# Other accumulator banks, another pool order, another tail, and another DMA queue in a hybrid encoder trunk

## The chip, the cores and the metric

The kernel runs on one core of one Trainium2 chip. The metric is the device time of one execution in microseconds. The time before is the median of three runs, 2415.16 us (2414.27 to 2418.61). TensorE does the matrix products, VectorE (DVE) and ScalarE (ACT) the elementwise work, GpSimd (POOL) small copies and stores, SyncE (SP) only requests transfers. A transfer is requested on the queue of one of SP, ACT or POOL and stands in that queue's order.

## The reference, cut to what matters

The input is 1024 frames of 1024 channels in float32, and there are two layers.

- Layer 0: RMSNorm, one input projection `w_in` (26 column tiles of 128), an RWKV-7 time-mixing group (8 heads of 64, a recurrence over time) beside a chunked band attention (8 heads of 64, softmax with a relative bias), both concatenated and mapped by `w_out`, residual; then RMSNorm, `square(relu(h @ up)) @ down` with 4096 hidden channels, residual.
- Layer 1: RMSNorm, pointwise product with GLU, causal depthwise convolution of 31 taps, LayerNorm, swish, pointwise product, residual; then the same MLP with other weights.
- A final RMSNorm: each frame is divided by the root mean square of its 1024 channels, times a gain per channel.

## The kernel before, in words

The sequence is cut into two halves of 512 frames, `h` = 0 and 1. Activations are kept transposed (128 channels by 512 frames, eight tiles `x` per half). Every float32 operand of a dense product is split into a rounded high part and the remainder (`wh`, `wl` of a weight; `xh`, `xl` of an activation), and each 128x128x512 step is three matmuls: high by high, low by high, high by low.

A dense weight goes through `weight_raw` (L247): a tile `wr` of 256 KB (four 128-row blocks of 128 columns, that is 512 B runs in memory; for the value projection 128 rows of 512 columns) with 4 buffers, requested on SP's queue. `weight_part` (L254) then makes `wh` on ACT (L258) and `wl` on DVE (L259), from a pool with 4 buffers each in the first part of the kernel (`wp1`) and 8 each in the later part (`wp2`). Such a half weight feeds 12 matmuls. `gemm` (L268) runs output tiles through the banks tagged `d`; L144 is the one line that issues every dense matmul.

The value projection is at the end of `w_in_gemm` (L397): its four output tiles of 128 frames each are held in four PSUM banks at once while `k` runs over eight weight tiles (L422 on). The banks' tags are in `SPARE`: d, d, a, a. The eight banks of the first part are d (2), w (2), v (1), c (1) and a (2). Tag `a` belongs to the attention, `c` holds the state of the RWKV recurrence for the whole of `rwkv(h)`, and `v` is used in passing by its second stage.

Order of the work: `w_in_gemm(0)`; then the mixed stage, in which `rwkv(0)` and `attention(0)` are laid between the dense steps of `w_in_gemm(1)`, and `rwkv(1)` and `attention(1)` between those of `mixer_out(0)` and `ffn(0)` of layer 0; then the wide part, whose products take two output tiles at a time (`wide[0]`) on five `d` banks: layer 0 for half 1, the convolution module and the MLP of layer 1 for both halves. The mixers hand their data on through DRAM: `pd`, `ph`, `pl`, `vd` from the projection, `yd` with their outputs, stored on POOL's queue and read on SP's. The small scratch transfers of the recurrence (`msc`, `nb`, `xsc`, `xdt`) and the attention's loads (`kk`, `qq`, `ql`, `vt`, `bias`) are on SP's queue too, between the weights.

The instruction order of each engine and queue is fixed when the program is built: a list scheduler takes instructions by priority ("support" first, then "mixer", "attn", "dense") against estimated costs. What runs later than it estimated is waited for in that order. Dense matmuls come in runs (L149 on, `run_of`), of 6 in the projections.

SBUF pools are stacked. A pool opened later at the same address waits, tile by tile (`reuse_waits="tile"`), for those that used it. The wide part opens `wp2` first, so its 32 KB per partition lie where `lop` and `wp1` and the first of `mp` (the MLP's intermediate tiles `mh`, `ml`) lay.

The tail is class `Out` (L1043). For each finished output tile `m`, `add` scales by the final gain (L1053), transposes back through bank `o` (L1059) and copies into row tiles `u` (L1065, L1067). The squares are summed on the way (`Stat.add`, L214: square on ACT, sum on DVE). In the last half the last tile comes in two column halves, and after each `write` (L1074) sums over channels by matmul (L1079), takes root (L1082) and reciprocal (L1083), scales the row tiles alternately on DVE (L1091) and ACT (L1089), and sends them out on SP's queue (L1092).

Of the kernel before, what the change touches and what calls it, by code (L numbers as in the profile page):

```python
# [64 lines left out]
def encoder_trunk(ctx: ExitStack, tc: tile.TileContext, x, vecs, consts, ext, w2a2, g2, w_in, w_out,  # L65
                  up0, dn0, pw1, pw2, up1, dn1, out):
    nc = tc.nc
# [8 lines left out]
    dram = ctx.enter_context(tc.tile_pool(name="dram", bufs=1, space=bass.MemoryType.DRAM))  # L76
    ps = {}
    wide = [False]
    wb = [None]
    extra = [None]  # L80
    deferred = []

    def psum(tag):
        return ps[tag].tile([P, T], F32, tag=tag, name=tag)
# [89 lines left out]
    def boost():  # L174
        return At("support")
# [4 lines left out]
    def tmp(tag="t1"):  # L180
        return dpool.tile([P, T], F32, tag=tag, name=tag)
# [65 lines left out]

    def weight_raw(src, n, queue=None):
        raw = wpool.tile([P, KH, P], F32, tag="wr", name="wr", bufs=4)
        (queue or nc.sync.dma_start)(raw[:].rearrange("p a b -> p (a b)").rearrange("p (k n) -> p k n", n=n),  # L250
                                     src.rearrange("(k p) n -> p k n", p=P))
        return raw

# [146 lines left out]
    def w_in_gemm(h, rhs, st, first=()):  # L400
        def evac(m, q, cols):
            rstd = st.rstd()
            s = tmp("t1")
            if Q0 <= m < K0:
                nc.vector.scalar_tensor_tensor(out=s[:], in0=q[:], scalar=0.125, in1=rstd[:],
                                               op0=ALU.mult, op1=ALU.mult)
            else:
                nc.vector.tensor_tensor(out=s[:], in0=q[:], in1=rstd[:], op=ALU.mult)  # L408
            ts = slice(h * T, (h + 1) * T)
            if Q0 <= m < V0:  # L410
                hi = tmp("t2")
                nc.scalar.copy(hi[:].bitcast(F32R), s[:])
                nc.vector.tensor_tensor(out=s[:].bitcast(F32R), in0=s[:], in1=hi[:], op=ALU.subtract)
                nc.gpsimd.dma_start(ph[m][:, ts], hi[:])
                stored[h, m] = nc.gpsimd.dma_start(pl[m][:, ts], s[:])
            else:
                stored[h, m] = nc.gpsimd.dma_start(pd[m][:, ts], s[:])

        run_of(RUN[0])
        gemm(w_in, 0, IN_ORDER, rhs, evac, st, first, mark=h)  # L420
        run_of(RUN[2])
        qs = [psum(tag) for tag in SPARE]  # L422
        for k in range(KT):
            with boost():
                hi, lo = (a[:].rearrange("p a b -> p (a b)")
                          for a in weight_part(w_in[k * P : (k + 1) * P, V0 * P : V0 * P + RW], RW))
            xh, xl = rhs[k]
            for t, q in enumerate(qs):
                ts = slice(t * P, (t + 1) * P)
                dense(q[:], xh[:, ts], hi, start=(k == 0), stop=False)  # L430
                dense(q[:], xl[:, ts], hi, start=False, stop=False)
                dense(q[:], xh[:, ts], lo, start=False, stop=(k == KT - 1))
        with boost():
            for t, q in enumerate(qs):
                s = tmp("t1")
                nc.scalar.activation(s[:], q[:], AF.Copy, scale=st.part[1][:, t : t + 1])
                nc.gpsimd.dma_start(vd[h * T + t * P : h * T + (t + 1) * P, :], s[:])
# [481 lines left out]

        gemm(w, row0, range(KT), rhs, evac, taper=taper, after=after, halves=halves)  # L920

    def norm_collect(xs, gname):
        st = Stat()
        rhs = [None] * KT

        def last(m, cols):
            if gname is not None:
                rhs[m] = split(xs[m][:], m, v(gname, m))
            st.add(xs[m][:], cols)

        return st, rhs, last

# [9 lines left out]
        return nrhs, st  # L942

    def ffn(xs, rhs, rst, up, dn, mp, nxt, out_to=None, late=None):
        st, nrhs, last = norm_collect(xs, nxt)
        if out_to is not None:
            out_to.st = st
        groups = DFF // D
        mids = [[None] * KT for _ in range(groups)]
        ahead = 2 if wide[0] else 0  # L950

        def evac(m, q, cols):
            rstd = rst.rstd()
            t = tmp("t1")
            nc.vector.scalar_tensor_tensor(out=t[:], in0=q[:], scalar=0.0, in1=rstd[:], op0=ALU.max, op1=ALU.mult)  # L955
            sq = tmp("t2")
            nc.scalar.activation(sq[:], t[:], AF.Square)  # L957
            hi = mp.tile([P, T], F32R, tag="mh", name="mh")
            nc.scalar.activation(hi[:], t[:], AF.Square)  # L959
            lo = mp.tile([P, T], F32R, tag="ml", name="ml")  # L960
            nc.vector.tensor_tensor(out=lo[:], in0=sq[:], in1=hi[:].bitcast(F32), op=ALU.subtract)  # L961
            mids[m // KT][m % KT] = (hi, lo)

        done = 0
        for grp in range(groups):
            end = grp == groups - 1
            if late is not None and end:
                with At("mixer"):
                    late()
# [75 lines left out]
    class Out:  # L1045
# [5 lines left out]
        def add(self, m, cols):  # L1051
            n = tmp("t1")
            nc.scalar.activation(n[:, cols], self.xs[m][:, cols], AF.Copy, scale=v("gf", m))  # L1053
            q = psum("o")
            c2, j = divmod(m, 4)
            ts = range(cols.start // P, cols.stop // P)
            for t in ts:
                with At("dense"):
                    nc.tensor.transpose(q[:, t * P : (t + 1) * P], n[:, t * P : (t + 1) * P], ident)  # L1059
            for t in ts:  # L1060
                if self.o[4 * c2 + t] is None:
                    self.o[4 * c2 + t] = self.op.tile([P, T + TAPS - 1], F32, tag="u", name="u", bufs=8)
                dst, src = self.o[4 * c2 + t][:, j * P : (j + 1) * P], q[:, t * P : (t + 1) * P]
                if t % 2:
                    nc.vector.tensor_copy(dst, src)  # L1065
                else:
                    nc.scalar.copy(dst, src)  # L1067
            if self.final and m == KT - 1:
                self.write(ts)

        def finish(self):
            with boost():
                self.write(range(4))

        def write(self, ts):
            q = psum("o")
            for t in ts:
                with At("dense"):
                    nc.tensor.matmul(q[:, t : t + 1], self.st.acc[:, t * P : (t + 1) * P], ones[:, 0:1], start=True, stop=True)  # L1079
            w = slice(ts[0], ts[-1] + 1)  # L1080
            r = self.r
            nc.scalar.activation(r[:, w], q[:, w], AF.Sqrt, bias=kc[:, 0:1], scale=1.0 / D)  # L1082
            nc.vector.reciprocal(out=r[:, w], in_=r[:, w])  # L1083
            for c2 in range(2):
                for t in ts:
                    rows = slice(self.h * T + t * P, self.h * T + (t + 1) * P)
                    o = self.o[4 * c2 + t][:, 0:T]
                    if t % 2:
                        nc.scalar.activation(o, o, AF.Copy, scale=r[:, t : t + 1])  # L1089
                    else:  # L1090
                        nc.vector.tensor_scalar(o, o, r[:, t : t + 1], None, op0=ALU.mult)  # L1091
                    nc.sync.dma_start(out[rows, c2 * T : (c2 + 1) * T], o)  # L1092


    with banks(d=2, w=2, v=1, c=1, a=2), tc.tile_pool(name="lop", bufs=1) as lop, tc.tile_pool(name="wp1", bufs=4) as wb[0]:
# [43 lines left out]

        with ExitStack() as es:  # L1140
            rp, ap, lp = (es.enter_context(tc.tile_pool(name=n, bufs=1, reuse_waits="tile")) for n in ("rp", "ap", "lp"))
            with At("mixer"):
                rwkv(0, rp, 3)
            with At("attn"):
                attention(0, ap)
            w_in_gemm(1, reload_x(1, lp), sb)
# [11 lines left out]

    wide[0] = True
    run_of(1)  # L1160
    with banks(d=5, w=1, o=2), tc.tile_pool(name="wp2", bufs=8, reuse_waits="tile") as wb[0], tc.tile_pool(name="mp2", bufs=10, reuse_waits="tile") as mp, tc.tile_pool(name="sx", bufs=4, reuse_waits="tile") as extra[0], tc.tile_pool(name="up", bufs=1, reuse_waits="tile") as up:
        dwt = up.tile([P, KT * TAPS], F32, tag="dwt", name="dwt")
        nc.scalar.dma_start(dwt[:], vecs[:, VOFF["dw"] : NVEC])
        halo = up.tile([P, KT, TAPS - 1], F32, tag="halo", name="halo")
# [92 lines left out]
```

## Time and profile before

| | us |
|---|---|
| median of three runs | 2415.16 |
| the profiled execution, its own time | 2409.59 |
| its span, first to last instruction | 2407.5 |
| TensorE busy | 2374.8 |
| VectorE busy | 1706.2 |
| ScalarE busy | 1198.9 |
| GpSimd busy | 117.1 |

The mean granted clock of TensorE is 0.998 of full speed. The profile is of one execution; the row views below are all taken from it. A busy TensorE still may run at half clock or with gaps that pipelining hides, so stretches are best compared by how many dense matmuls they hold.

### The profile page before, as it was taken

The page shows a single profiled execution, that of the slowest core. Times are in us where ns is not written, and L with a number is a line of the kernel's source. Part 1 is how long each engine was busy: PE and PEld are TensorE (multiplying, and loading weights), DVE is VectorE, ACT ScalarE, POOL GpSimd, SP SyncE. Part 2 cuts the span into 40 slices and gives each one's busy share as a digit, 9 for nine tenths or more (in the row PEclk, how much of TensorE's full clock was granted, in tenths as well). Part 3 has the DMA queues.
Part 4 walks back from the last instruction along what each step waited for, and adds up shares of the span by engine and source line. Part 5 has one row for each costly group of instructions (what it writes and reads, how often), then busy time and mean ns, then how long its engine had stood idle before and what let it go on. Part 6 is the DMA issues. An engine that isn't in the chain of part 4 may idle for free.

```text
span 2407.5 us, 37122 instructions
## 1 busy us (share of the span) xinstructions
PE 2374.8 (99%) x12804; PEld 1956.4 (81%) x12804; DVE 1706.2 (71%) x3575; ACT 1198.9 (50%) x2323; POOL 117.1 (5%) x243
## 2 busy tenths in 40 slices
PE   9999999899999999999999999999999999999998
PEld 7777777788888888888888888888888888888887
DVE  6787776587777764579999746799997465434434
ACT  6567666677676753434433335334333365423324
POOL 1120111100000000011000000000000000000000
PEclk9999999999999999999999999999999999999999
DMA  8574445633343323453333334433333334333332
GB/s 260 163 217 139 120 121 171 188 102 115 93 120 110 90 74 90 145 166 92 101 97 97 97 97 135 123 94 97 96 98 99 95 112 140 97 97 97 97 98 67
DMA packets 476042, 283.34 MB, mean 118 GB/s; under 512 B 44512, under 2 KB 453216, under 8 KB 475856
## 3 DMA queue, kind: packets, MB, share of 16 engines
q1 hardware_dynamic: 464976, 249.46, 35.7%
q0 software_dynamic: 9488, 30.28, 3.6%
q8 instruction: 101, 1.65, 0.3%
q10 hardware_dynamic: 1392, 1.24, 0.2%
q14 instruction: 85, 0.70, 0.1%
HBM read 247.31 MB, written 36.72 MB: 118 GB/s over the span
## 4 chain that ended last, share of the span: by engine, by line
PE 88%; DVE 4%; DMA 3%; ACT 3%; issue 1%; SPq 1%; ACTq 0%; DVEq 0%
PE d L144 77%; DMA pt<-pd 1%; PE a L160 1%; PE v L688 1%; PE a L883 1%; DVE wl L259 1%; PE a L144 1%; ACT wh L258 1%; PE a L861 1%; PE a L863 1%; PE c L746 1%; PE c L740 0%; DVE pr L650 0%; PE c L736 0%; PE v L676 0%
## 5 line engine op out<-in xcount | busy, mean ns | idle before, releaser
L258 ACT CAST wh<-wr 128x512 fp32r<-128x512 f32 x744 | 460.1, 620 | 922.9 <-PE d L144 839.0
L144 PE MATMUL d<-xh,wh 128*128 128x512 f32 x1872 | 745.6, 398 | 0.3 <-DVE t L408 0.2
L144 PE MATMUL d<-xh,wl 128*128 128x512 f32 x1872 | 730.7, 391 | 0.9 <-DVE wl L259 0.9
L144 PE MATMUL d<-xl,wh 128*128 128x512 f32 x1872 | 730.2, 390 | 0.0
L259 DVE TENSOR_TENSOR wl<-wr,wh 128x512 fp32r<-128x512 f32 x744 | 503.4, 687 | 197.5 <-ACT wh L258 142.2
L144 PEld LDWEIGHTS d<-xh,wl 128*128 128x128 f32 x1872 | 351.7, 188 | 76.4 <-DVE wl L259 1.3
L144 PEld LDWEIGHTS d<-xh,wh 128*128 128x128 f32 x1872 | 352.2, 188 | 70.0 <-issue 1.2
L144 PEld LDWEIGHTS d<-xl,wh 128*128 128x128 f32 x1872 | 352.3, 188 | 67.7 <-issue 0.5
L144 PE MATMUL d<-mh,wh 128*128 128x512 f32 (+1 forms) x1040 | 405.8, 390 | 0.0
L144 PE MATMUL d<-mh,wl 128*128 128x512 f32 (+1 forms) x1040 | 401.8, 386 | 0.0
L144 PE MATMUL d<-ml,wh 128*128 128x512 f32 (+1 forms) x1040 | 401.6, 386 | 0.0
L1014 DVE SCALAR_TENSOR_TENSOR cv<-u,dwt,cv 128x512 f32<-128x512 f32 x480 | 332.7, 749 | 0.7
L144 PEld LDWEIGHTS d<-mh,wl 128*128 128x128 f32 x1040 | 195.4, 188 | 40.0
L144 PEld LDWEIGHTS d<-ml,wh 128*128 128x128 f32 x1040 | 195.6, 188 | 37.6
L144 PEld LDWEIGHTS d<-mh,wh 128*128 128x128 f32 x1040 | 195.5, 188 | 37.7
L913 DVE TENSOR_TENSOR x<-d,x 128x512 f32<-128x512 f32 (+1 forms) x146 | 97.8, 681 | 152.1 <-PE d L144 151.6
L955 DVE SCALAR_TENSOR_TENSOR t<-d,rstd 128x512 f32<-128x512 f32 x128 | 86.6, 688 | 114.6 <-PE d L144 111.9
L961 DVE TENSOR_TENSOR ml<-t,mh 128x512 fp32r<-128x512 f32 x128 | 87.9, 689 | 12.6 <-ACT mh L959 9.5
L957 ACT ACTIVATE t<-t 128x512 f32<-128x512 f32 x128 | 80.0, 625 | 12.2 <-DVE t L955 11.2
L959 ACT ACTIVATE mh<-t 128x512 fp32r<-128x512 f32 x128 | 78.9, 616 | 0.0
L745 ACT ACTIVATE sd<-vs,dc 64x64 f32<-64x64 f32 x128 | 44.1, 345 | 40.7 <-DVE vs L749 29.6
L221 DVE TENSOR_TENSOR acc<-acc,t 128x512 f32<-128x512 f32 (+1 forms) x86 | 58.0, 675 | 8.4 <-ACT t L220 8.3
(271 smaller groups left out, 2335.0 us busy)
## 6 DMA issues: line engine op xcount, KB each, us to landing
wr<-in_up_dram SPq DMA_DIRECT2D x256, 256.0 KB
wr<-in_dn_dram SPq DMA_DIRECT2D x256, 256.0 KB
wr<-in_w_in_dram SPq DMA_DIRECT2D x103, 256.0 KB
wr<-in_pw_dram SPq DMA_DIRECT2D x96, 256.0 KB
wr<-in_w_out_dram SPq DMA_DIRECT2D x32, 256.0 KB
pd<-t POOLq DMA_DIRECT2D x28, 256.0 KB, 2.6
x<-xd SPq DMA_DIRECT2D x24, 256.0 KB
pt<-pd SPq DMA_DIRECT2D x42, 128.5 KB
```

Of the source, the lines that this page charges most:

```text
L144: ins = nc.tensor.matmul(*a, **k)
L160: ins = issue(*a, **k)
L221: nc.vector.tensor_tensor(out=self.acc[:, cols], in0=self.acc[:, cols], in1=sq[:, cols], op=ALU.add)
L258: nc.scalar.copy(hi[:], raw[:])
L259: nc.vector.tensor_tensor(out=lo[:], in0=raw[:], in1=hi[:].bitcast(F32), op=ALU.subtract)
L745: nc.scalar.activation(sd[hs[hd], :], sv[hs[hd], hd, c, :], AF.Copy, scale=dc[hs[hd], c : c + 1])
L913: nc.vector.tensor_tensor(out=xs[m][:, cols], in0=q[:, cols], in1=xs[m][:, cols], op=ALU.add)
L955: nc.vector.scalar_tensor_tensor(out=t[:], in0=q[:], scalar=0.0, in1=rstd[:], op0=ALU.max, op1=ALU.mult)
L957: nc.scalar.activation(sq[:], t[:], AF.Square)
L959: nc.scalar.activation(hi[:], t[:], AF.Square)
L961: nc.vector.tensor_tensor(out=lo[:], in0=sq[:], in1=hi[:].bitcast(F32), op=ALU.subtract)
L1014: nc.vector.scalar_tensor_tensor(out=c[:], in0=u[:, tap : tap + T], scalar=dw(tap), in1=c[:], op0=ALU.mult, op1=ALU.add)
```

## The change

There are four edits.

1. In `w_in_gemm(1)` the value projection takes the banks d, d, v, c and no longer d, d, a, a.
2. From the start of the mixed stage until the wide part, `weight_raw` requests on POOL's queue and no longer on SP's. These are 196 transfers of 256 KB: 52 of `w_in_gemm(1)`, 16 of `mixer_out(0)`, 64 and 64 of `ffn(0)`.
3. The wide part opens its pools in the order `up`, `mp2`, `sx`, `wp2`; before it was `wp2`, `mp2`, `sx`, `up`.
4. The tail of the last half: for the last output tile the squares are made on DVE and not added to `acc`; the matmul over channels takes both parts. These sums, with root and reciprocal, stand ahead of the last transposes. Of the four row tiles of a column half DVE scales three (ACT the second), and the second and third are sent on ACT's queue.

```diff
+            mixed[0] = True                    # at the start of the mixed stage
     def weight_raw(src, n, queue=None):
         raw = wpool.tile([P, KH, P], F32, tag="wr", name="wr", bufs=4)
-        (queue or nc.sync.dma_start)(raw[:]...
+        (queue or (nc.sync if wide[0] or not mixed[0] else nc.gpsimd).dma_start)(raw[:]...
...
-        qs = [psum(tag) for tag in SPARE]
+        qs = [psum(tag) for tag in (SPARE if h == 0 else ("d", "d", "v", "c"))]
...
-    with banks(d=5, w=1, o=2), tc.tile_pool(name="wp2", bufs=8, ...) as wb[0], tc.tile_pool(name="mp2", bufs=10, ...) as mp, tc.tile_pool(name="sx", bufs=4, ...) as extra[0], tc.tile_pool(name="up", bufs=1, ...) as up:
+    with banks(d=5, w=1, o=2), tc.tile_pool(name="up", bufs=1, ...) as up, tc.tile_pool(name="mp2", bufs=10, ...) as mp, tc.tile_pool(name="sx", bufs=4, ...) as extra[0], tc.tile_pool(name="wp2", bufs=8, ...) as wb[0]:
...
     # norm_collect, last(m, cols)
-            st.add(xs[m][:], cols)
+            if final and m == KT - 1:
+                sq = tmp("t2")
+                nc.vector.tensor_tensor(out=sq[:, cols], in0=xs[m][:, cols], in1=xs[m][:, cols], op=ALU.mult)
+                st.rest = sq
+            else:
+                st.add(xs[m][:], cols)
...
     # Out.add: before q = psum("o") and the transposes
+            if self.final and m == KT - 1:
+                self.sums([self.st.acc, self.st.rest], ts)
...
+        def sums(self, parts, ts):
             q = psum("o")
+            pairs = [(part, t) for part in parts for t in ts]
+            for i, (part, t) in enumerate(pairs):
                 with At("dense"):
+                    nc.tensor.matmul(q[:, t : t + 1], part[:, t * P : (t + 1) * P], ones[:, 0:1],
+                                     start=(i == 0), stop=(i == len(pairs) - 1))
             # root on ACT, reciprocal on DVE as before
...
         def write(self, ts):
+            for i, (c2, t) in enumerate((c2, t) for c2 in range(2) for t in ts):
-                    if t % 2:
+                if i == 1 if self.final else t % 2:
                     nc.scalar.activation(o, o, AF.Copy, scale=r[:, t : t + 1])
                 else:
                     nc.vector.tensor_scalar(o, o, r[:, t : t + 1], None, op0=ALU.mult)
-                    nc.sync.dma_start(out[rows, c2 * T : (c2 + 1) * T], o)
+                queue = nc.scalar if self.final and i in (1, 2) else nc.sync
+                queue.dma_start(out[rows, c2 * T : (c2 + 1) * T], o)
```

## Rows read from the trace of the kernel before

**Rows 1.** First part of the page: engine, busy us, share of span, instructions.
```profile
PE 2374.8 (99%) x12804; PEld 1956.4 (81%) x12804; DVE 1706.2 (71%) x3575; ACT 1198.9 (50%) x2323; POOL 117.1 (5%) x243
```

**Rows 2.** Stretches: from:to, length, busy us per engine (instructions), granted clock, DMA share, GB/s.
```profile
200.00:429.40 229.40, 223.35 (x1700) 180.12 (x1699) 171.12 (x549) 157.31 (x378) 31.70 (x69) 0.99 0.47 138
429.40:464.60 35.20, 29.86 (x149) 23.25 (x148) 16.96 (x39) 21.80 (x44) 4.90 (x15) 0.95 0.57 182
464.60:955.80 491.20, 486.78 (x3346) 401.56 (x3345) 351.27 (x1004) 325.64 (x682) 17.54 (x47) 1.00 0.36 103
955.80:1027.90 72.10, 71.22 (x315) 58.59 (x313) 38.11 (x59) 31.04 (x52) 6.67 (x18) 1.00 0.49 144
```

**Rows 3.** Timeline of TensorE around the value projection of half 1: start, duration, [idle before].
```profile
427.15 0.59 PE L783 MATMUL c<-sg,g2s 128*128 128x256 f32 x2
429.49 0.39 PE L144 MATMUL d<-wh,xh 128*128 128x512 f32 x1
436.55 0.88 PE L160 MATMUL a<-pT,vt 128*64 128x128 f32 x12 [0.57 <-ACT pT L884]
441.89 1.27 PE L883 MATMUL a<-cst,pt 128*128 128x128 f32 x8 [3.32 <-ACT pt L874]
443.88 1.97 PE L160 MATMUL a<-pT,vt 128*64 128x128 f32 x16 [0.73 <-ACT pT L884]
445.79 0.80 PE L144 MATMUL a<-wh,xh 128*128 128x512 f32 x1
481.80 0.55 PE L705 MATMUL v<-cst,bk 128*128 128x128 f32 x3
```

**Rows 4.** Stretches, as Rows 2: inside the stall, and in the wide part.
```profile
440.00:450.00 10.00, 7.38 (x40) 5.92 (x41) 2.14 (x8) 5.58 (x12) 2.44 (x7) 0.83 0.04 14
1200.00:1300.00 100.00, 100.00 (x443) 82.82 (x442) 99.79 (x158) 33.08 (x56) 3.61 (x3) 1.00 0.33 97
```

**Rows 5.** Timelines of VectorE and GpSimd: last use of bank c, last attention output, its store.
```profile
427.78 0.42 DVE L784 TENSOR_TENSOR e<-e,c 128x256 f32<-128x256 f32 x1
445.91 0.29 DVE L894 COPY yo<-a 128x128 f32<-128x128 f32 x1 [4.49 <-PE a L160]
446.49 0.54 POOL L895 DMA_DIRECT2D yd<-yo  x1 [7.87 <-DVE yo L894]
```

**Rows 6.** Requests by tile (KB each, median us to landing), and SP's of weights, 200 to 1027 us.
```profile
pd<-t POOLq DMA_DIRECT2D x28, 256.0 KB, 2.6
g2s<-in_g_dram POOLq DMA_DIRECT2D x1, 256.0 KB, 7.9
...
L250 SPq DMA_DIRECT2D wr<-in_dn_dram x64: 367/378/805, 565.1 to 1006.2; - x64
L250 SPq DMA_DIRECT2D wr<-in_w_in_dram x46: 333/390/1303, 201.1 to 431.0; - x46
```

**Rows 7.** GpSimd: its pd stores (ns min/median/max), and the waits of its attention stores (us, times, longest).
```profile
L417 POOL DMA_DIRECT2D pd<-t x28: 539/539/573, 34.6 to 351.8; - x28
...
POOL yd L895 <- DVE yo L894: 175.0, 21, 25.2
```

**Rows 8.** Timelines of VectorE and TensorE at the first weights of the wide part.
```profile
1027.21 1.28 DVE L259 TENSOR_TENSOR wl<-wr,wh 128x512 fp32r<-128x512 f32 x2
1027.95 0.50 PE L144 MATMUL d<-xh,wl 128*128 128x512 f32 x1 [0.93 <-DVE wl L259]
```

**Rows 9.** Timeline of all engines after the last dense matmul (it ends at 2399 us).
```profile
2399.52 0.42 ACT L220 ACTIVATE t<-x 128x256 f32<-128x256 f32 x1 [1.69 <-DVE x L913]
2399.84 0.49 ACT L1053 ACTIVATE t<-x,vec 128x256 f32<-128x256 f32 x1
2400.66 0.50 PE L1079 MATMUL o<-ones,acc 128*128 128x1 f32 x4
2401.20 0.26 ACT L1082 ACTIVATE orst<-o,small 128x2 f32<-128x2 f32 x1
2401.70 0.88 DVE L1091 TENSOR_SCALAR u<-u,orst 128x512 f32<-128x512 f32 x2
```

More of the change, by code (lines that the diff above doesn't have):

```diff
@@ L78, in encoder_trunk @@
     wide = [False]
+    mixed = [False]
     wb = [None]
@@ L249, in weight_raw @@
         raw = wpool.tile([P, KH, P], F32, tag="wr", name="wr", bufs=4)
-        (queue or nc.sync.dma_start)(raw[:].rearrange("p a b -> p (a b)").rearrange("p (k n) -> p k n", n=n),
+        (queue or (nc.sync if wide[0] or not mixed[0] else nc.gpsimd).dma_start)(raw[:].rearrange("p a b -> p (a b)").rearrange("p (k n) -> p k n", n=n),
                                      src.rearrange("(k p) n -> p k n", p=P))
@@ L920, in residual_gemm, with norm_collect @@
         gemm(w, row0, range(KT), rhs, evac, taper=taper, after=after, halves=halves)
-    def norm_collect(xs, gname):
+    def norm_collect(xs, gname, final=False):
         st = Stat()
@@ L944, in ffn @@
     def ffn(xs, rhs, rst, up, dn, mp, nxt, out_to=None, late=None):
-        st, nrhs, last = norm_collect(xs, nxt)
+        st, nrhs, last = norm_collect(xs, nxt, out_to is not None and out_to.final)
         if out_to is not None:
@@ L1053, in add @@
             nc.scalar.activation(n[:, cols], self.xs[m][:, cols], AF.Copy, scale=v("gf", m))
-            q = psum("o")
             c2, j = divmod(m, 4)
             ts = range(cols.start // P, cols.stop // P)
+            if self.final and m == KT - 1:
+                self.sums([self.st.acc, self.st.rest], ts)
+            q = psum("o")
             for t in ts:
@@ L1069, in add @@
                 self.write(ts)
[L1071 to L1075, printed above, removed]
+        def sums(self, parts, ts):
             q = psum("o")
-            for t in ts:
+            pairs = [(part, t) for part in parts for t in ts]
+            for i, (part, t) in enumerate(pairs):
                 with At("dense"):
-                    nc.tensor.matmul(q[:, t : t + 1], self.st.acc[:, t * P : (t + 1) * P], ones[:, 0:1], start=True, stop=True)
+                    nc.tensor.matmul(q[:, t : t + 1], part[:, t * P : (t + 1) * P], ones[:, 0:1],
+                                     start=(i == 0), stop=(i == len(pairs) - 1))
             w = slice(ts[0], ts[-1] + 1)
@@ L1083, in write, with finish @@
             nc.vector.reciprocal(out=r[:, w], in_=r[:, w])
[L1084 to L1087, printed above, removed]
-                    if t % 2:
-                        nc.scalar.activation(o, o, AF.Copy, scale=r[:, t : t + 1])
-                    else:
-                        nc.vector.tensor_scalar(o, o, r[:, t : t + 1], None, op0=ALU.mult)
-                    nc.sync.dma_start(out[rows, c2 * T : (c2 + 1) * T], o)
+        def finish(self):
+            with boost():
+                self.sums([self.st.acc], range(4))
+                self.write(range(4))
+        def write(self, ts):
+            r = self.r
+            for i, (c2, t) in enumerate((c2, t) for c2 in range(2) for t in ts):
+                rows = slice(self.h * T + t * P, self.h * T + (t + 1) * P)
+                o = self.o[4 * c2 + t][:, 0:T]
+                if i == 1 if self.final else t % 2:
+                    nc.scalar.activation(o, o, AF.Copy, scale=r[:, t : t + 1])
+                else:
+                    nc.vector.tensor_scalar(o, o, r[:, t : t + 1], None, op0=ALU.mult)
+                queue = nc.scalar if self.final and i in (1, 2) else nc.sync
+                queue.dma_start(out[rows, c2 * T : (c2 + 1) * T], o)
     with banks(d=2, w=2, v=1, c=1, a=2), tc.tile_pool(name="lop", bufs=1) as lop, tc.tile_pool(name="wp1", bufs=4) as wb[0]:
@@ L1160, in encoder_trunk @@
     run_of(1)
-    with banks(d=5, w=1, o=2), tc.tile_pool(name="wp2", bufs=8, reuse_waits="tile") as wb[0], tc.tile_pool(name="mp2", bufs=10, reuse_waits="tile") as mp, tc.tile_pool(name="sx", bufs=4, reuse_waits="tile") as extra[0], tc.tile_pool(name="up", bufs=1, reuse_waits="tile") as up:
+    with banks(d=5, w=1, o=2), tc.tile_pool(name="up", bufs=1, reuse_waits="tile") as up, tc.tile_pool(name="mp2", bufs=10, reuse_waits="tile") as mp, tc.tile_pool(name="sx", bufs=4, reuse_waits="tile") as extra[0], tc.tile_pool(name="wp2", bufs=8, reuse_waits="tile") as wb[0]:
         dwt = up.tile([P, KT * TAPS], F32, tag="dwt", name="dwt")
```

## The prediction

> **What bounds the kernel now.** I read the first part of the page, then the busy time by stretches, then the timeline of TensorE wherever a stretch shows it idle, then the waits. TensorE is busy for 2374.8 us of a span of 2407.5 us [rows 1], so 32.7 us of idle time is nearly all that an edit of order, banks or queues can win, beside time at half clock. Of it 6.1 us lie in the stretch 200 to 429 us, 5.3 us in 429 to 465 us, 4.4 us in 465 to 956 us and 0.9 us in 956 to 1028 us (length less busy time in each line) [rows 2]. The wide part is saturated: in its 100 us from 1200 on TensorE has no idle time at 443 matmuls, 0.226 us each [rows 4]. The mixers are not the bound of the mixed stage: after 955.8 us dense matmuls run alone for 72 us [rows 2], so what is won on TensorE earlier comes through to the end.
>
> The dense spot is the value projection of half 1. It begins at 429.49 us on its two `d` banks and cannot go on: the two `a` banks are the attention's, which still works through its last block. TensorE waits 0.57 us, 3.32 us and 0.73 us for ACT and only at 445.79 us enters bank `a` [rows 3]. In the 10 us from 440 us the granted clock is 0.83 of full speed: it fell to its lower level, 1.2 GHz, for a third of them, behind the 3.32 us of idle time [rows 3, 4].
>
> **Edit 1, the banks.** It removes the wait on `a`. Bank `c` is last written by TensorE at 427.15 us and last read by DVE at 427.78 plus 0.42, that is 428.2 us, before the projection starts at 429.49 us [rows 3, 5]. Bank `v` is used again at 481.80 us only, by the next half's recurrence [rows 3]. So the 96 matmuls (4 tiles, 8 steps, 3 each), 96 x 0.226 = 21.7 us, can run on while the attention ends between them. Saved: 0.57 + 3.32 + 0.73 = 4.62 us of waiting, and the clock's loss, 0.17 x 10 us = 1.7 us [rows 3, 4], of which I count 1.6, since TensorE idled for a little of it. Together 6.2 us. Nothing is computed less.
>
> What is late next? `mixer_out(0)` needs the attention's last output, copied at 445.91 us and stored from 446.49 us [rows 5]. With the projection running between its three steps (transposes, copy, product), each step may wait for one run of six matmuls, 6 x 0.226 = 1.4 us, so the copy comes at about 446 + 4 = 450 us. A store takes 0.54 + 2.6 us [rows 6, 7], a load I put at the same, the split at two operations of 0.6: ready at 458 us. The projection would now end at 464.6 - 6.2 = 458.4 us [rows 2], and that operand is the last of eight, used 21 matmuls (4.7 us) later. It just fits; were it late by its whole three runs, 4 us of the 6.2 would be gone. Bounds of edit 1: a gain of 2 to 8 us.
>
> **Edit 2, the queue.** 196 weight requests leave SP, each 0.38 us there [rows 6], 75 us in all; they come to POOL. The waits of TensorE name no weight in the mixed stage, so this frees SP's queue for the mixers' small transfers, and what it can win is bounded by the idle time of these stretches without edit 1's, 6.1 + 4.4 = 10.5 us [rows 2]. Its cost on POOL: a store of 256 KB takes 0.539 us [rows 7], so 196 x 0.54 = 106 us beside the 61 us (31.7 + 4.9 + 17.5 + 6.7) that POOL is busy in these 828 us [rows 2]. No row shows such a request in 512 pieces, where `pd` has 128 rows; at four times 0.54, 2.2 us, it would be 423 us of POOL, still half of the time. Landing: 2.6 us for `pd`, 7.9 us for the slowest load on that queue [rows 6]. Against this stands the lead. From 201.1 to 1006.2 us SP requested about 190 weights [rows 6] (the code's 196 less the first six), one per 4.2 us; four `wr` buffers make 17 us from request to reuse, less 7.9 us of landing at worst and 1.3 us of splitting: about 8 us of slack, 13 at a landing of 2.6. Behind a weight on POOL now stand the stores of `pd`, `ph`, `yd`, the copies `dc`, the clearing of `bias`; they lose at most the few requests ahead of them. Ahead of a weight stand the same, and they wait for DVE: the attention's stores 175.0 us in 21 waits, 8.3 us on average, 25.2 at most [rows 7]. Most of that is POOL with nothing else to do, and TensorE's fixed order carries the mixers and the dense work together, so a store is rarely late against the weight behind it. I take 0, the ends being a gain of 5 and a loss of 20 us.
>
> **Edit 3, the pools.** At 1026.6 us TensorE has two of the first three matmuls of the wide part done and then waits 0.93 us for a `wl` made at 1027.21 us [rows 8]; DVE makes it only then because its tile lies where tiles of the last MLP were read to the end. With `wp2` last it lies in space that the mixers left by 955.8 us, and `up`, which now takes the old place, is filled later. Gain 1.0 us; bounds 0 and 1.6 (the wait and a slow restart).
>
> **Edit 4, the tail.** After the last dense matmul the chain was add, square (starts 2399.52), gain (2399.84), transposes, sums (2400.66), root (2401.20), reciprocal, scaling (2401.70) [rows 9]. Without the square on ACT the gain starts 0.32 us earlier; with sums ahead of the transposes the root comes about 0.5 us earlier and runs beside them. The first scaling then starts at about 2401.1, and the transfers, 1 MB at the end, follow it. DVE scales three tiles (0.44 us each, two took 0.88 us [rows 9]), behind a stream that takes longer. Gain 0.6 us; bounds 1.0 and a loss of 0.3 where ACT's own requests delay it.
>
> **The sum.** 6.2 + 0 + 1.0 + 0.6 = 7.8 us. From the profiled execution's 2409.6 us that gives 2401.8 us. The median of the runs shown lies 5.6 us above the profiled one, and I carry that along: 2415.2 - 7.8 = 2407.4, rounded 2407.5 us.
>
> **The rivals.**
> *The stall moves.* Edit 1 only shifts the wait to the attention's last output or the next mixers' first matmuls. For it: the margin above is nearly nil, and TensorE also idles where the next mixers start. Against it: eight steps of cover. Gain 2 + 0.5, with 3 and 4 as forecast or half: about 2412 us, no measurable change.
>
> *SP was the brake.* With weights gone from it, the mixers' transfers come earlier and half of the 10.5 us goes too: 2407.5 - 5 = 2402.5 us. Against it: the waits in these stretches are for ACT and DVE by the rows shown, not for transfers.
>
> *Weights late on POOL (slower).* A weight stands behind an attention store that waits for DVE. The point from which it decides is the slack of 8 to 13 us: a wait of 25.2 us [rows 7] costs 25.2 - 10 = 15 us of dense work, plus 2 us of half clock each. One gives 2407.5 + 17 = 2424 us, two 2441 us. For it: by the code weights now share a queue with 24 stores of mixer outputs in each half. Against it: the fixed order of TensorE.
>
> *POOL held up by DVE (slower).* A request on POOL would stretch while DVE is in a long instruction. The 28 `pd` stores took 539 to 573 ns [rows 7] in stretches where DVE is busy for 75% [rows 2], so it is not visible. If it came at DVE's three quarters to each of 196 requests with half of an operation of 0.64 us (two took 1.28 us [rows 8]), 0.75 x 196 x 0.32 = 47 us of POOL would be added, of which between nothing (all inside the slack) and all would show; at a third it is 2407.5 + 16 = 2423 us. The Trainium skill, "SBUF — State Buffer", section "SBUF: two separate sides", states the like: while DVE runs an operation that takes both of its ports, GpSimd cannot write descriptors, and such transfers should move to SP's or ACT's queue. By that rule edit 2 goes the wrong way; the rows on `pd` do not show it.
>
> **How the numbers follow.** Forecast (edits 1, 3, 4 win, 2 neutral): 0.52, own range 2403 to 2411. Stall moves: 0.18. SP was the brake: 0.13. Weights late on POOL: 0.14. Held up by DVE: 0.03. What this measurement can tell from no change is 0.2%, 4.8 us. Faster: 0.47 of the forecast's 0.52, 0.12 of SP's, 0.02 of the moved stall, 0.61. Slower: 0.17 of the last two less 0.03 of short waits, 0.14. Same: 0.25. The range runs from 2401 us, below the second rival, to 2419 us, a third of the way beyond the moved stall to the late weights; about 0.05 lie below and 0.13 above.
>
> **What would show it.** Right: the matmuls of the projection in `v` and `c` with no wait over 0.5 us from 429 to 465 us, the granted clock at 1.00 there, the stage's end 6 us earlier; no 0.93 us wait at the first `wl` of the wide part; root ahead of the last copies. Wrong: `wh` (L258) waiting for a transfer of `wr` in the mixed stage, TensorE waiting for `wl`, POOL's requests well over 1 us, or new half-clock stretches.

## The result and the profile after

The changed kernel takes 2435.12 us (median of 4 runs, 2434.26 to 2438.64) beside 2415.95 us for the kernel before (4 runs on the same chip): ratio 1.0081, 95% interval 1.0064 to 1.0099. Slower by 19 us, where 8 us less were forecast. The profiled execution took 2435.3 us at a span of 2433.44 us, 26.0 us more than the 2407.45 us of the profiled one of before.

The page's first part, the line of the engines, answers to [rows 1]: TensorE is busy for 23.2 us more and idle for 2.8 us more, so nearly all of the loss is not waiting. GpSimd's 196 more instructions are the weights' requests.

```profile
PE 2398.0 (99%) x12812; PEld 1957.2 (80%) x12812; DVE 1711.8 (70%) x3577; ACT 1189.1 (49%) x2315; POOL 255.2 (10%) x439
```

Stretches of the kernel after, columns as in [rows 2]; the second is the value projection of half 1, from its begin to its end, the last is the stretch of [rows 4] in the wide part.

```profile
200.00:429.80 229.80, 224.67 (x1732) 182.23 (x1729) 168.37 (x543) 152.92 (x370) 64.36 (x114) 0.99 0.46 137
429.80:458.90 29.10, 28.93 (x159) 22.80 (x158) 15.49 (x38) 19.01 (x43) 9.66 (x15) 1.00 0.55 182
...
1200.00:1300.00 100.00, 100.00 (x436) 81.62 (x435) 98.98 (x156) 31.91 (x54) 2.62 (x3) 1.00 0.33 95
```

The second line is the stage that the forecast turned on: 29.1 us for 35.2, idle 0.17 us for 5.3, a granted clock of 1.00 for 0.95. In the third, TensorE has no idle time and the same clock as before, and does 436 matmuls where [rows 4] has 443. So the matmuls follow one another more slowly.

How that looks in the timeline of TensorE, in the same stretch, of the kernel before and then of the kernel after (start, duration):

```profile
1199.78 0.39 PE L144 MATMUL d<-xh,wh 128*128 128x512 f32 x1
1200.01 0.39 PE L144 MATMUL d<-xl,wh 128*128 128x512 f32 x1
1200.24 0.39 PE L144 MATMUL d<-xh,wl 128*128 128x512 f32 x1
...
1202.50 0.39 PE L144 MATMUL d<-xh,wh 128*128 128x512 f32 x1
```

```profile
1199.74 0.39 PE L145 MATMUL d<-xl,wh 128*128 128x512 f32 x1
1199.97 0.40 PE L145 MATMUL d<-xh,wl 128*128 128x512 f32 x1
1200.21 0.39 PE L145 MATMUL d<-xh,wh 128*128 128x512 f32 x1
...
1202.54 0.39 PE L145 MATMUL d<-xl,wh 128*128 128x512 f32 x1
```

Twelve steps from start to start take 2.72 us before (226.7 ns each) and 2.80 us after (233.3 ns). The column to read is the start: the duration is modelled and hides it. Only the means of many durations show a little of it. Grouped by form over 1050 to 2390 us (count, then busy us and mean ns), before and after:

```profile
L144 PE MATMUL d<-xh,wl 128*128 128x512 f32 x1186 | 461.7, 389 | 0.0
L144 PE MATMUL d<-mh,wl 128*128 128x512 f32 x752 | 292.6, 389 | 0.0
```

```profile
L145 PE MATMUL d<-xh,wl 128*128 128x512 f32 x1193 | 473.0, 396 | 0.0
L145 PE MATMUL d<-mh,wl 128*128 128x512 f32 x723 | 281.3, 389 | 0.0
```

Only products with `xh` and `xl` are slow; those with the MLP's intermediates `mh` and `ml`, on weights of the same pool, are as before. And not all with `xh` and `xl`: of the eight pairs `xh`, `xl` (one for each input tile), the first two lie in the pool `sx`, which edit 3 moves along with the weights. In the wide part a product with one of the other six pairs is followed by the next start after 233 to 235 ns on average, one with the first two after 231 and 229 ns; before, all are at 227. Later stretches start later, so fewer products with `mh` fall into this window after.

Where the 26.0 us lie, by the first dense matmul of each stage in the two timelines: up to `w_in(1)` +5.0, `w_in(1)` −4.7 (these two pass time between them), the value projection −5.9, `mixer_out(0)` +0.1, `ffn(0)` +11.6, the wide part +20.7 (1372.56 to 1393.22), after the last dense matmul −0.8. The mixers' small products move between the stages of the first layer; taken together, from the first value projection to the wide part, these are 4.5 us longer, little more than what two executions of one order differ by there (the table behind the experiments).

### The profile page after: what moved, and what is told of

Its sections match the earlier page's. It is cut to its first block, busy times and chain, and to the rows that moved or that the text cites. A ratio compares the mean times of both kernels' runs of the same rounds, so it can differ in the third digit from the quotient of the medians.

```text
span 2433.4 us, 37142 instructions
## 1 busy us (share of the span) xinstructions
PE 2398.0 (99%) x12812; PEld 1957.2 (80%) x12812; DVE 1711.8 (70%) x3577; ACT 1189.1 (49%) x2315; POOL 255.2 (10%) x439
## 4 chain that ended last, share of the span: by engine, by line
PE 85%; DVE 4%; DMA 3%; ACT 2%; issue 2%; SPq 0%; POOL 0%; DVEq 0%; ACTq 0%; POOLq 0%
PE d L145 75%; DMA pt<-pd 1%; PE v L689 1%; PE a L161 1%; PE a L884 1%; DVE wl L260 1%; PE a L862 1%; ACT wh L259 1%; PE c L741 1%; PE a L864 0%; PE c L747 0%; PE c L737 0%; DMA nb<-msc 0%; PE v L677 0%; PE c L762 0%
## 5 line engine op out<-in xcount | busy, mean ns | idle before, releaser
L145 PE MATMUL d<-xh,wl 128*128 128x512 f32 x1872 | 740.5, 396 | 0.0
L145 PE MATMUL d<-xl,wh 128*128 128x512 f32 x1872 | 737.8, 394 | 0.0
L251 POOL DMA_DIRECT2D wr<-in_up_dram x64 | 47.9, 749 | 185.8 <-DVE wl L260 139.8
L251 POOL DMA_DIRECT2D wr<-in_dn_dram x64 | 48.0, 750 | 167.1 <-DVE wl L260 112.7
```

The lines of the kernel that those rows point to most:

```text
L145: ins = nc.tensor.matmul(*a, **k)
L251: (queue or (nc.sync if wide[0] or not mixed[0] else nc.gpsimd).dma_start)(raw[:].rearrange("p a b -> p (a b)").rearrange("p (k n) -> p k ...
```

## The experiments

The theory after this look: the two operands of a matmul in the wide part no longer start alike. In what follows an operand is called displaced when its start, in bytes within a partition, differs from that of the other one modulo 128. `up` holds a tile of 8 x 31 floats (992 bytes per partition) and one of 8 x 30 (960), together 15 x 128 + 32 bytes. Opened last, it moved nobody; opened first, it puts `mp2`, `sx` and `wp2` 32 bytes past a multiple of 128, while `xh` and `xl` of the small pool, opened long before, stay on a multiple. These starts come from the tile sizes in the code, for the traces show no addresses; in the programs as built they are as said. The rivals: the weights' queue, or the order of the pools itself, by waits.

**pad**: the kernel after, padded by 96 bytes.

```diff
-        dwt = up.tile([P, KT * TAPS], F32, ...)
-        nc.scalar.dma_start(dwt[:], ...)
+        dwt = up.tile([P, KT * TAPS + 24], F32, ...)
+        nc.scalar.dma_start(dwt[:, 0 : KT * TAPS], ...)
```

> The changed kernel, with 96 bytes added to the first small tile of the wide part's first pool, so that every pool opened behind it starts on a multiple of 128 bytes again (in the changed kernel they start 32 bytes past one). Theory P, placement: the wide part lost 20.7 us (from its first dense matmul to its last 1393.2 us, 1372.6 before) because xh and xl lie on multiples of 128 while the weights do not; so here it takes 1371 to 1374 us and the median is 2414 us (2410 to 2418). Rival Q, weights late on POOL: nothing of the queue changes, 2435 us (2431 to 2439). Rival O, the pools' order itself makes waits: also 2435 us.

Measured: 2410.51 us, ratio to the kernel before 0.9997 (0.9985 to 1.0008). The wide part takes 1371.3 us, 1.2 less than before, and the matmuls are back to their old rate, in the same order on TensorE as in the kernel after. In the wide part 96 bytes are worth 21.9 us (1393.2 to 1371.3); by the two ratios to the kernel before they are worth 0.84%, some 20 us.

```profile
1200.00:1300.00 100.00, 100.00 (x442) 82.83 (x442) 99.78 (x158) 33.27 (x57) 3.61 (x3) 1.00 0.33 96
```

**order**: the kernel before with edit 3 alone (the four pools in the new order).

> The kernel before with the new pool order alone; the wide pools then start 32 bytes past a multiple of 128. P: about 20 us slower, 2436 us (2432 to 2440), the wide part about 1392 us, matmuls with xh and xl at 231 to 237 ns each and those with mh and ml at 227. Q: no loss without the queue, 2415 us. O: slower too, but by idle time of TensorE and not by matmuls that follow each other more slowly.

Measured: 2435.54 us, 1.0088 (1.0071 to 1.0105); wide part 1393.2 us, with no idle time. Edit 3 makes the whole loss by itself.

**shift32**: the kernel before, its pools in the old order, with an unused 32-byte tile ahead of them.

```diff
-    with banks(d=5, w=1, o=2), tc.tile_pool(name="wp2", ...
+    with banks(d=5, w=1, o=2), tc.tile_pool(name="gap", bufs=1, ...) as gap, tc.tile_pool(name="wp2", ...
+        nothing = gap.tile([P, 8], F32, tag="gap", name="gap")
+        nc.gpsimd.memset(nothing[:], 0.0)
```

> The kernel before, its pool order kept, with an unused tile of 32 bytes ahead of the wide part's pools, so that weights, mh, ml and the first two xh and xl all move by 32 bytes. P: 20 us slower, 2436 us (2432 to 2440), as with the new order. O and Q: no change, 2416 us (2413 to 2419).

Measured: 2433.99 us, 1.0083 (1.0066 to 1.01); wide part 1392.4 us. So it is not the order of the pools but the start of the tiles; TensorE's order is that of before.

**gap32**: the same tile between `wp2` and `mp2`: weights back on a multiple of 128, `mh` and `ml` moved by 32.

> The kernel before with an unused tile of 32 bytes between the weights' pool of the wide part and the pools behind it: weights stay on a multiple of 128, mh, ml and the first two of xh and xl move 32 bytes off. If what counts is that the two operands of a matmul stand differently to that grid: matmuls with mh and ml follow each other at 231 to 237 ns and not 227, those with xh and xl mostly at 227; by the counts (2352 with mh or ml, about 816 with the moved xh, 6.7 ns each) the wide part takes 1372.6 + 21 = 1393 us, median 2434 us. If what counts is the weights' own place: no change, 2413 us.

Measured: 2435.29 us, 1.0104 (1.0088 to 1.0119); wide part 1395.1 us for the 1393 expected. The slow kind changes sides, as these groups over 1050 to 2390 us show (the two pairs `xh`, `xl` in `sx` moved too, and they lift the mean of that kind over 389):

```profile
L144 PE MATMUL d<-xh,wl 128*128 128x512 f32 x1198 | 468.7, 391 | 0.0
L144 PE MATMUL d<-xl,wh 128*128 128x512 f32 x1198 | 467.8, 390 | 0.0
L144 PE MATMUL d<-mh,wl 128*128 128x512 f32 x718 | 283.6, 395 | 0.0
```

**shift64**: as shift32 with a tile of 64 bytes.

> The kernel before, with an unused tile of 64 bytes per partition ahead of the wide part's pools, whose order stays (the tile is cleared once on GpSimd). The weights of the wide part then start 64 bytes past a multiple of 128 and the split activations xh, xl of the small pool stay on multiples of 128, a relative offset of 64 instead of the 32 of the earlier run with 32 bytes (1.0083). Theory A, what counts is the start within a block of 64 bytes: nothing changes, ratio 0.999 to 1.002 (about 2412 us), dense matmuls with xh and xl at 226 to 227 ns each in the wide part, 443 in the 100 us from 1200 on. Theory B, within a block of 128 bytes: slow as with 32 bytes, ratio 1.007 to 1.010 (about 2433 us), these matmuls at 231 to 237 ns, about 436 in that stretch.

Measured: 2435.03 us, 1.0089 (1.0071 to 1.0108); wide part 1392.2 us; theory B in so far as a block of 64 bytes is ruled out. Again `xh`, `xl` are slow and `mh`, `ml` are not:

```profile
L144 PE MATMUL d<-xl,wh 128*128 128x512 f32 x1195 | 470.5, 394 | 0.0
L144 PE MATMUL d<-ml,wh 128*128 128x512 f32 x725 | 282.2, 389 | 0.0
```

**all32**: a 32-byte tile ahead of the small pool, so that all operands of the dense products move together.

> The kernel before, with an unused tile of 32 bytes per partition opened ahead of the small pool and of every later pool, so that the weights, the split activations and the intermediate tiles all move by 32 bytes together, in the mixed stage as in the wide part: each starts 32 bytes past a multiple of 128 and none is displaced against another. Theory A, the two operands of a matmul must start alike: no loss, ratio 0.998 to 1.002 (about 2412 us), 443 matmuls in the 100 us from 1200 on at 226 to 227 ns. Theory B, each operand must start on a multiple of 128 bytes: slower everywhere, in the wide part by at least the 20 us of the runs with one operand displaced and in the mixed stage by some 10 more, ratio 1.009 to 1.02, 436 matmuls or fewer in that stretch.

Measured: 2414.65 us, 1.0014 (0.9999 to 1.0028); wide part 1372.7 us; theory A. Every dense operand starts 32 bytes past a multiple of 128 and the rate is that of before:

```profile
1200.00:1300.00 100.00, 100.00 (x442) 82.80 (x442) 99.77 (x158) 34.09 (x58) 3.61 (x3) 1.00 0.32 95
```

What counts is therefore the start of the one operand against the other, not of either alone: a displacement of 32 or of 64 bytes costs, none costs nothing. By the intervals between starts from 1200 to 1300 us, products of displaced operands mostly follow at 230 to 238 ns (32 bytes) and at 233 to 234 ns (64 bytes), the others at 226 to 227. That the grid is one of 128 bytes is not shown: in the programs as built, operands that are not displaced also agree modulo 512, and no run displaced one by 128 or 256 bytes.

With placement settled, the other three edits were taken one by one.

**sp**: the kernel after with the weights' requests back on SP.

> The changed kernel with the weights of the mixed stage back on SP's queue. From the start of the first value projection to the wide part it took 860.3 us against 855.8 before, although the second value projection alone got 5.9 us shorter; P with a costly queue: the 10 us come back, 2425 us (2421 to 2430), the wide part stays at 1393 us. P with a neutral queue: 2435 us. Q: all of the loss is the queue's, 2409 us (2405 to 2413).

Measured: 2435.2 us, 1.0088 (1.0073 to 1.0103), the same as the kernel after (1.0081) within the intervals: beside edit 1 the queue makes no difference that the medians show. The wide part stays at 1393.2 us. The stage in front of it is 853.7 us for 860.3 (more on that behind the table).

**banks**: the kernel before with edit 1 alone.

```diff
-        qs = [psum(tag) for tag in SPARE]
+        qs = [psum(tag) for tag in (SPARE if h == 0 else ("d", "d", "v", "c"))]
```

> The kernel before with edit 1 alone, banks d, d, v, c. If the stall's removal pays as forecast and what ate it in the changed kernel was the queue: the second value projection takes about 29 us (35.0 before), and from the first value projection to the wide part 849.6 us (855.8 before); median 6 us below before, about 2407 us. Rival, the stall moves: the projection is as short, but the stage is 853 to 856 us long and the median within 3 us of before.

Measured: 2412.73 us, 1.0001 (0.9991 to 1.0011). The projection shrinks from 35.0 to 26.9 us with no idle time, and by the interval at most 2.2 us of it are left at the end. In the timelines (VectorE, SP's queue, TensorE of this kernel) the gain goes as follows:

```profile
449.97 0.29 DVE L894 COPY yo<-a 128x128 f32<-128x128 f32 x1 [1.27 <-PE a L160]
```

```profile
440.28 12.79 SPq L250 DMA_DIRECT2D wr<-in_w_out_dram  x4
453.23 0.38 SPq L938 DMA_DIRECT2D mh<-yd  x1
453.66 0.90 SPq L482 DMA_DIRECT2D pt<-pd  x2
```

```profile
463.37 0.39 PE L543 MATMUL w<-xl,lora 128*128 128x256 f32 x1 [0.99 <-DVE xl L525]
465.39 0.39 PE L543 MATMUL w<-xl,lora 128*128 128x256 f32 x1 [1.52 <-DVE xl L525]
```

The attention's last output comes at 449.97 us for 445.91 [rows 5], as forecast. SP stands at four weights that wait for buffers until 453.23 us; behind them comes the load of that output, and behind both the loads `pt` of the next mixers, whose first products TensorE then waits for (2.5 us in two waits). It does not wait for the split of that late output. Its idle time goes from 5.3 to 0.0 us in the projection, from 1.3 to 4.5 in `mixer_out(0)` and from 3.1 to 6.0 in `ffn(0)`; over the mixed stage it is 16.9 us in both kernels.

**queue**: the kernel before with edit 2 alone.

> The kernel before with edit 2 alone, the mixed stage's weights on GpSimd's queue. If the queue costs: the stage from the first value projection to the wide part takes 859 to 862 us against 855.8, median 2417 us (2415 to 2420). If it is neutral: within 3 us of before. If weights came late as in the slower rival of the prediction: TensorE waits for wl in that stage, 2425 us or more.

Measured: 2430.45 us, 1.0078 (1.0055 to 1.0102). By the time this is the case of late weights, but its sign is absent: TensorE waits for no `wl` in the stage, which takes 874.7 us. Alone, edit 2 costs 19 us, as idle time of 29.3 us in the mixed stage and 20.5 us at half clock (before: 16.9 and 6.8). Half of it is seen in one place: the order written for it leaves more of the attention to be done when the projection begins (62 matmuls of the attention for 46, among them 8 more products with `vt`), and without edit 1 the projection still waits for bank `a`: it takes 44.5 us for 35.0. The other half is spread over the stages around it and was not followed up. TensorE's waits in the projection, and the stretch (0.85 is the granted clock):

```profile
447.99 1.54 PE L884 MATMUL a<-cst,pt 128*128 128x128 f32 x6 [2.74 <-ACT pt L875]
450.15 1.55 PE L161 MATMUL a<-pT,vt 128*64 128x128 f32 x12 [0.62 <-ACT pT L885]
456.90 1.73 PE L884 MATMUL a<-cst,pt 128*128 128x128 f32 x8 [3.19 <-ACT pt L875]
```

```profile
430.00:475.00 45.00, 36.59 (x173) 27.69 (x172) 20.84 (x57) 22.92 (x50) 12.78 (x27) 0.85 0.52 167
```

**best**: the kernel with padding and the weights on SP (edits 1, 3 aligned, 4).

> The changed kernel with both repairs: 96 bytes of padding, and the weights on SP's queue. The padded one was at 2410.5 us with a stage of 857.0 us, the one on SP's queue without padding had 853.7 us in that stage. If the queue costs 3 us or more: 2407 us (2404 to 2409). If it is neutral: 2410.5 us (2409 to 2413).

Measured: 2409.65 us, 0.9990 (0.9981 to 0.9999): in the range of the neutral queue, and not told apart from **pad** (0.9997).

**last_on_pool**: that kernel with one load moved.

```diff
-                nc.sync.dma_start(t[:], yd[k]...)
+                (nc.gpsimd if h == 0 and k == KT - 1 else nc.sync).dma_start(t[:], yd[k]...)
```

> The combination run before (edits 1, 3 with 96 bytes of padding, 4; weights on SP), with one change: the last load of the first half's mixer outputs goes on GpSimd's queue, behind the store that it waits for, and no longer on SP's ahead of the next attention's loads. Theory A, what gives edit 1's gain back is that SP stands at that load and at weights in front of the next mixers' loads: TensorE's idle time from the second projection on falls by 2 to 4 us, ratio to the kernel before 0.997 to 0.9985 (that run had 0.9990). Theory B, the mixers' chain from the last attention output on is late whatever the queue, or weights alone hold SP: no change from that run, ratio 0.9985 to 0.9995, the waits for the next attention's first operands remain.

Measured: 2403.87 us, 0.9961 (0.9949 to 0.9973), the fastest of all. Timelines of GpSimd and of SP in this run, then SP's in **best**:

```profile
451.93 0.56 POOL L944 DMA_DIRECT2D mh<-yd  x1 [1.98 <-DMA yd<-yo]
```

```profile
451.98 0.98 SPq L483 DMA_DIRECT2D pt<-pd  x2
```

```profile
455.76 0.38 SPq L944 DMA_DIRECT2D mh<-yd  x1
456.20 0.90 SPq L483 DMA_DIRECT2D pt<-pd  x2
```

The load leaves at 451.93 us for 455.76, `pt` at 451.98 for 456.20. But the projection began at 428.71 us here and at 432.38 in **best**: counted from there, `pt` leaves 0.5 us earlier and no more, for SP stands at two weights before it. TensorE's idle time in `mixer_out(0)` does fall, from 5.2 to 2.3 us, the amount that theory A gave, without theory A's step; `ffn(0)` is 4.4 us shorter as well, of which only 1.5 us are idle time. Moving one load made the scheduler write another order for much of the first layer's second half, and the gain lies in that order; which part of it, is open. The two traces differ by 11 us, the medians by 5.8, the ratios to the kernel before by 0.29% (7 us).

**pad_last**: the same load moved in the kernel with padding, where the weights are on GpSimd's queue.

> All four edits with 96 bytes of padding (2410.5 us, ratio 0.9997), with the last load of the first half's mixer outputs on GpSimd's queue, where the weights are by edit 2, and not on SP's, so that SP holds no load that waits for the last attention output. In the run with padding SP went on at 459.3 us only, and TensorE waited 2.24 us for the first product of the next mixers. Theory A, SP's order at that load gives edit 1's gain back: the next mixers' loads leave SP 10 to 15 us earlier, TensorE's idle time in the first layer's output projection falls from 4.5 to about 2 us, and the time by 1 to 3 us: ratio 0.9985 to 0.9993. Theory B, the chain of the mixers itself is late, or a load on GpSimd holds the weights behind it: no gain, ratio 0.9995 to 1.001.

Measured: 2416.62 us, 1.0013 (1.0002 to 1.0023): theory A's step came and its gain did not. `pt` leaves SP 9.7 us after the projection's begin (442.58 us) and no longer 32.0, and the 2.24 us wait is gone. But on GpSimd the load stands behind stores of `vd` that wait for ACT, and goes 34.7 us after that begin, 3.1 later than in **pad**; TensorE waits 2.54 us, for 0.96, for its split:

```profile
467.03 0.54 POOL L438 DMA_DIRECT2D vd<-t  x1 [0.94 <-ACT t L437]
467.56 0.54 POOL L944 DMA_DIRECT2D mh<-yd  x1
```

```profile
471.49 0.50 PE L145 MATMUL d<-xh,wh 128*128 128x512 f32 x1 [2.54 <-ACT xh L189]
```

Of the 7.1 us between the two traces 4.3 lie in `w_in(1)`, ahead of the first instruction whose order on TensorE differs. The kernels with the order of before show 223.4 to 225.3 us in that part, so some of this may be the difference from one execution to the next; the rest is open.

All of the mixed stage in one table, from the records of TensorE (us; the stage runs from the first value projection to the wide part; the rest is the length less idle time less half of the time at half clock):

| | length | idle | at half clock | rest |
|---|---|---|---|---|
| before | 855.8 | 16.9 | 6.8 | 835.5 |
| after | 860.3 | 20.1 | 10.2 | 835.1 |
| pad | 857.0 | 18.7 | 6.8 | 834.9 |
| banks | 854.8 | 16.9 | 6.8 | 834.4 |
| sp | 853.7 | 15.9 | 6.8 | 834.4 |
| queue | 874.7 | 29.3 | 20.5 | 835.2 |
| best | 854.7 | 17.5 | 3.4 | 835.5 |
| last_on_pool | 847.4 | 13.2 | 3.4 | 832.5 |
| pad_last | 863.7 | 22.6 | 13.7 | 834.3 |

The rest is the same but for one kernel: every edit of banks, queues and order here but **last_on_pool** moves idle time and what the clock loses behind it, and nothing else.

Each line is one execution. Six kernels have the same order on TensorE up to the wide part (before, **order**, **shift32**, **gap32**, **shift64**, **all32**), and theirs take 855.7 to 859.6 us in this stage, so a difference of under 4 us between two lines is no finding. The three kernels with edits 1 and 2 (after, **pad**, **pad_last**: 857.0 to 863.7) are longer than the three with edit 1 and the weights on SP (**banks**, **sp**, **best**: 853.7 to 854.8). They share a wait at the begin of `ffn(0)` that the other three do not have, for the norm's root (`rc`), and 6.8 us at half clock from there on. In the kernel after:

```profile
527.74 1.12 PE L239 MATMUL d<-cst,rc 128*128 128x128 f32 x4 [2.28 <-ACT rc L232]
```

So edit 2 beside edit 1 probably costs a few us in the mixed stage; the medians of the whole kernel (after against **sp**, **pad** against **best**) do not show it.

## Why the prediction was wrong

**The step that failed** is the price of edit 3: "Gain 1.0 us; bounds 0 and 1.6". The gain is there: the 0.93 us wait of [rows 8] is gone, and with the padding the wide part is 1.2 us shorter than before. But the same edit displaced the weights by 32 bytes against the `xh` and `xl` of the small pool, and the wide part takes 20.7 us more (1393.2 for 1372.6). About 2700 of its 6000 matmuls have displaced operands, and each is followed some 7 ns later than before. I asked when the space comes free and not where the tiles start. The lower bound of nothing had no reason behind it: no row of before shows a displaced operand, so its cost was unknown on that side. Among the rivals for a slower result there was none of this kind; the sum of tile sizes (992 + 960 bytes) was in the code, beside a rounding to 32 floats that other tiles get.

**Edit 1** did on the spot what was written: no wait over 0.5 us, the clock at 1.00, the stage's end at 458.90 us for the forecast 458.4, the last attention output at 449.97 in **banks** for the forecast 450. What failed is the step from there to the end, that 6.2 us come through. The first rival, that the stall moves, took the gain back (1.0001, 0.9991 to 1.0011), at the places it named. I had reckoned with the eight dense steps that use the late operand last, and not with the next mixers' inputs, which stand on SP behind weights and behind that operand's load. "It just fits" was read too tightly: ready at 458 us and used at 458.4 + 4.7 = 463.1 us, the operand had 5 us to spare, and in **banks** TensorE does not wait for it. In the changed kernel it does. There the order written with edit 2 puts more of the attention beside the projection, the last output comes at 457.51 us and not at 450, and TensorE waits for its split and then for the next mixers' load:

```profile
465.75 0.50 PE L145 MATMUL d<-xh,wh 128*128 128x512 f32 x1 [1.45 <-ACT xh L189]
477.62 0.39 PE L862 MATMUL a<-kk,qq 128*128 128x320 f32 x1 [2.24 <-DMA pt<-pd]
```

**Edit 2** at 0 was right in the sum as far as the medians tell and wrong as a statement on its own: no difference beside edit 1 (**sp** against the kernel after), a loss of 19 us without it (**queue**), at the far end of the bounds. In so far as that loss was traced, it comes by a mechanism that was not among the rivals: the order built for the edit, not late weights. Of the rivals on GpSimd neither came. A weight's request takes 0.75 us, between the 0.54 and 2.2 us that I had as bounds, and lands after 3.3 to 3.7 us (medians). The group of the `up` weights on GpSimd (200 to 1030 us; the idle times are ahead of its requests) and its longest wait:

```profile
L251 POOL DMA_DIRECT2D wr<-in_up_dram x64 | 47.9, 749 | 185.8 <-DVE wl L260 139.8 <-DVE zs L739 14.3 <-DVE vs L742 10.9
```

```profile
POOL wr L251 <- DVE wl L260: 333.9, 114, 10.7
```

GpSimd mostly waits for the tile to come free, that is for the previous weight's split, and no wait of TensorE names a weight. The longest request of a weight is 0.78 us, so none was held up for a VectorE operation of 0.64 us, with VectorE busy for 69% of that part. The rule of the Trainium skill ("SBUF — State Buffer", section "SBUF: two separate sides") that GpSimd cannot write descriptors while VectorE runs an operation that takes both of its ports does not show here. That does not refute it, for the trace does not say which of VectorE's operations took both ports. Of the signs against the forecast two did come, both small: `wh` waits once for a weight of the mixed stage (2.2 us, and 2.3 in **sp**, so not for the queue), and there is the new half-clock stretch in `ffn(0)`.

**Edit 4** came as forecast: from the last dense matmul to the end 8.5 us before, 7.7 after. The gain and the square now start together (0.32 us apart in [rows 9]), the sums stand ahead of the transposes, the root follows:

```profile
2426.22 0.42 DVE L932 TENSOR_TENSOR t<-x 128x256 f32<-128x256 f32 x1
2426.22 0.51 ACT L1059 ACTIVATE t<-x,vec 128x256 f32<-128x256 f32 x1 [1.03 <-DVE x L914]
2426.70 0.61 PE L1084 MATMUL o<-ones,t 128*128 128x1 f32 x4 [0.64 <-DVE t L932]
2427.17 0.42 PE L1067 MATMUL o<-cst,t 128*128 128x128 f32 x2
2427.35 0.26 ACT L1088 ACTIVATE orst<-o,small 128x2 f32<-128x2 f32 x1 [0.61 <-PE o L1084]
```

Without the displacement the forecast would still have been too good: the kernel with padding has 2410.5 us (0.9997), the case "The stall moves", by the 6 us of edit 1.

One reading in the chances is off as well: 2419 us, the upper end of the range, is 7 of the 12 us from the moved stall (2412) to the late weights (2424), not a third.

## What to carry to other kernels

When a change reorders or resizes pools, add up the bytes ahead of each operand of the matmuls: pad the small tiles so that the pools behind them keep their place on the grid (here 96 bytes made 1952 into 2048), and look at the starts of matmuls one after another, since a busy TensorE shows no wait for it. A stall removed by another bank is won only if what follows in the same queues comes early too: say what stands in the queue behind the late operand's load, and behind requests that wait for a buffer. An order that is planned anew makes two edits' costs depend on each other, so run each alone and both together.

## What the runs showed of the hardware

Dense products of 128x128 by 128x512 in split float32 follow one another after 226 to 227 ns when the two operands start alike (modulo 128 bytes, and here modulo 512 too), and mostly after 230 to 238 ns when the one is displaced against the other by 32 or 64 bytes, whichever of the two it is (**shift32**, **gap32**); it does not matter whether they start on a multiple of 128 (**all32**). The granted clock is 1.00 in both, and **pad** and the kernel after have the same instructions on TensorE in the same order. Why is open: no view of the trace shows what such a matmul waits for. Displacements under 32 bytes, of 96 (modulo 128) and of 128 or 256 were not run.
